# Moving the first RMSNorm behind the first product, and merging two score matmuls, in a two-layer hybrid decoder on one core

## The chip, the cores and the metric

The kernel runs on one core of one Trainium2 chip. The metric is device time in microseconds (us) of one execution. The engines are the TensorE (PE in the profile, its weight loads PEld), the VectorE (DVE), the ScalarE (ACT), GpSimd (POOL) and the SyncE (SP), which here only issues DMA transfers. Each engine works its instructions in the order in which the kernel wrote them, and waits where an operand or a buffer is not ready.

## The reference

Two layers, one sequence of 256 tokens, 1024 channels, float32. Cut to what matters here:

```python
for l in range(DEPTH):                               # DEPTH = 2
    h = rmsnorm(x, norm_mix_g[l])                    # x * rsqrt(mean(x*x) + eps) * g
    x = x + mixer_block(h, w_in[l], ...)             # mLSTM and sliding-window attention, gated
    h = rmsnorm(x, norm_mlp_g[l])
    x = x + square(relu(h @ w_up[l])) @ w_down[l]
return rmsnorm(x, final_norm_g)

# mixer_block
proj = h @ w_in                                      # 6664 columns: mqk, mv, mo, gates mi/mf, aq, ak, av, ga, gb
mqk = silu(causal_conv(mqk, conv_w, conv_b))         # q and k of the mLSTM
logf = log_sigmoid(mf + b_fgate)                     # and its running sums and maxima: the gates
hm = mlstm(mq, mk, mv, mi + b_igate, logf)           # normed per head, times sigmoid(mo)
# attention: 16 query heads of 64, 4 key/value heads, window 128, a sink per head, a T5 bias
logits = q @ k.T / 8 + bias                          # masked to 0 <= distance < 128
m = max(max(logits), sink); p = exp(logits - m)
ha = p @ v / (sum(p) + exp(sink - m))
y = sigmoid(ga) * (hm @ w_branch_m) + sigmoid(gb) * (ha @ w_branch_a)
return y @ w_out
```

A factor that is one number per token, such as the norm's rsqrt, can be applied to a product's rows after the product as well as to x before it. The factor g is one number per channel and has to be applied before.

## The kernel before

**Precision.** Float32 operands of the large products are split in two parts, hi (a cast, on ACT) and lo (what is left, a subtraction on DVE). A product is then three matmuls: hi by hi, hi by lo, lo by hi. This holds for the weights (`pump_hi`, `pump_lo`, lines 142 and 123) and for the activations (`evac_split`, line 311).

**Weights.** They stream from memory in pieces of 128 rows by 1024 columns (512 KB). SP loads a piece into one of 4 `raw` buffers (`pump_dma`, line 114), ACT casts it into a hi buffer, DVE writes lo and thereby frees the raw buffer for the load of the piece four later. There are 7 pairs of hi and lo buffers; a pair is free again when PE has used it.

**Slots.** The products are cut into slots, mostly 24 matmuls of 256 columns or 12 of 512 columns. `run_slots` (line 191) writes the instructions of one slot after the other, and this sets the order on every engine: first the side work hung to the slot with `at`; then the hi casts of pieces up to four ahead of what the slot needs (`limits` can hold that back); then the work hung with `at_late`; the lo parts; the work hung with `at_last`; then the slot's matmuls (units); then what was hung behind it with `after`.

The stages of a layer's mixer are, with their slots: mv (8 slots, the values of the mLSTM), kv (4: keys, values and gate columns), aq (8: queries), qk (8), mo (8), gb, ga (8 each), then the branches. `s_mv`, `s_kv`, `s_aq`, `s_qk` are their first slots. In an `xs` unit (line 211) tokens stand in the output's partitions, in a `ws` unit (line 226) channels. A group's head and tail say in which order its units run: "k" uses up one weight piece per slot, all four output banks in turn; "t" runs the first token tile over two pieces at a time and then the second tile; "b" finishes one output bank per slot; "p" pairs them.

**The start** (`setup_start`, line 401, and `first_norm`, line 526). SP loads X's first tile of 128 tokens in two halves, the g row, three weight pieces, X's second tile, a fourth piece, and then eleven small tensors, some of them broadcast to 128 partitions by the load. PE runs dummy matmuls on zeros meanwhile (`N_WARM`). Squares of a tile are summed on ACT and DVE, POOL takes the power -1/2, DVE scales the tile, PE transposes it in blocks of 128, and ACT and DVE write the hi and lo parts with g as a factor per partition, block by block. The first product (mv) takes the first tile first.

**The gates.** `gates1` computes log sigmoid with a chain of small operations on POOL, with one reciprocal on DVE in it. `gates2`, `gates2b`, `gates2c` transpose the result on PE and scan it on DVE; `gates3` transposes back and writes the gate columns. In POOL's order `k_split` (the lo part of the keys) comes ahead of `gates1`.

**The heads.** Each of 16 heads runs in four steps. `att1` (line 827): the scores, four matmuls, then bias and minimum on DVE, exponentials on ACT. `att2`: sums and reciprocal on DVE, scaling on POOL. `att3`: transposes on PE and their copy. `att4`, for four heads: the product with the values. `heads_at` (line 884) gives the slot of `att1`, counted from `s_qk`; `att2` comes one slot later, `att3` three. The four score matmuls of a head are:

```python
nc.tensor.matmul(sp[:, 0:P], q[:, 0:P], kh[:, gk, 0:P], start=True, stop=False, ...)
nc.tensor.matmul(sp[:, 0:P], q[:, 0:P], kl[:, gk, 0:P], start=False, stop=True, ...)
nc.tensor.matmul(sp[:, P : 3 * P], q[:, P:T], kh[:, gk, :], start=False, stop=False, ...)
nc.tensor.matmul(sp[:, P : 3 * P], q[:, P:T], kl[:, gk, :], start=False, stop=True, ...)
```

Tiles named `pa` and `pb` in the profile are PSUM banks, four of each.

Of the kernel before, what the change touches and what calls it, by code (L numbers as in the profile page):

```python
# [11 lines left out]
F32 = mybir.dt.float32  # L12
# [5 lines left out]
P = 128  # L18
# [24 lines left out]
def trunk(ctx: ExitStack, tc: tile.TileContext, x, norm_mix_g, w_in, conv_w, conv_b, b_igate, b_fgate,  # L43
# [43 lines left out]
    def piece(w, kt, c0):  # L87
        def load(raw):
            nc.sync.dma_start(raw[:, :1024], w[kt * P : (kt + 1) * P, c0 : c0 + 1024])

        pieces.append((load, 1024))
        return len(pieces) - 1
# [21 lines left out]
    def pump_dma():  # L114
        j = n_dma[0]
        if j < len(pieces):
            raws[j] = wp.tile([P, 1040], F32, tag="raw", bufs=N_RAW, name=nm("raw"))
            pieces[j][0](raws[j])
            n_dma[0] += 1
# [3 lines left out]
    def pump_lo():  # L123
# [5 lines left out]
        los.clear()  # L129

# [256 lines left out]
    N_WARM = (26, 16, 8)  # L387

    def small_loads():
# [4 lines left out]
        for l in range(DEPTH):  # L394
            nc.sync.dma_start(gb_bias[:, l, 0:4], b_igate[l].partition_broadcast(P))
            nc.sync.dma_start(gb_bias[:, l, 4:8], b_fgate[l].partition_broadcast(P))
            nc.sync.dma_start(sink[:, l, :], attn_sinks[l].partition_broadcast(P))
            nc.sync.dma_start(rows[40 * l : 40 * l + 32, :], conv_w[l].rearrange("j (m c) -> (j m) c", c=P))
            nc.sync.dma_start(rows[40 * l + 32 : 40 * l + 40, :], conv_b[l].rearrange("(m c) -> m c", c=P))

    def setup_start():
        grow = big8()[:8, 0, 0:P]
        nc.sync.dma_start(X[:, 0, 0:512], xv[:, 0, 0:512])
        nc.sync.dma_start(X[:, 0, 512:], xv[:, 0, 512:])
        nc.sync.dma_start(grow, norm_mix_g[0].rearrange("(k c) -> k c", c=P))
        for i in range(N_RAW):
            if i == 3:
                nc.sync.dma_start(X[:, 1, :], xv[:, 1, :])
            pump_dma()
# [7 lines left out]
        pw = psA()  # L417
        for _ in range(N_WARM[0]):
            nc.tensor.matmul(pw[:, :P], mask, mask, start=True, stop=True)
        pg = psA()  # L420
        nc.tensor.transpose(pg[:, :8], grow, ident[:8, :8])
        S0["gcol"] = const.tile([P, KT], F32, name="gcol")
        S0["pg"], S0["pw"] = pg, pw
        for _ in range(N_WARM[1]):
            nc.tensor.matmul(pw[:, :P], mask, mask, start=True, stop=True)

    def setup_small():
# [6 lines left out]
        nc.scalar.copy(Rs, z[:, 0:384])  # L434
        for r in (0, 32):
            nc.gpsimd.affine_select(out=z[r : r + 32, 0:4], in_=z[r : r + 32, 0:4], pattern=[[-1, 4]],
                                    compare_op=ALU.not_equal, fill=1.0, base=0, channel_multiplier=1)
        nc.scalar.copy(sel, z[:, 0:4])

    def setup_cols():  # L440
        pt = psB()
        nc.tensor.transpose(pt[:, :80], S0["rows"], ident[:80, :80])
        nc.vector.tensor_copy(cw, pt[:, :80])
        pt = psB()
        nc.tensor.transpose(pt[:16, :NB_BUCKETS], S0["rb"], ident[:NB_BUCKETS, :NB_BUCKETS])
        nc.vector.tensor_scalar(nsink, sink, -1.0, None, op0=ALU.mult)
        rbT = const.tile([16, NB_BUCKETS], F32, name="rbT")
        nc.vector.tensor_scalar(rbT, pt[:16, :NB_BUCKETS], -1.0, None, op0=ALU.mult)
# [77 lines left out]
    def first_norm(st, xtag, nxt):  # L526

        xh, xl = st["hT"] = xT_tiles(xtag)
        N = [Norm(0), Norm(1)]
        gcol, xn, pts = S0["gcol"], {}, {}  # L530

        def scale(tt, hf):
            xn[tt, hf] = tmp()
            nc.vector.tensor_scalar(xn[tt, hf], X[:, tt, hc(hf)], N[tt].r[:, :1], None, op0=ALU.mult)

        def tr(tt, hf):
            pts[tt, hf] = psB()
            for j in range(4):
                nc.tensor.transpose(pts[tt, hf][:, j * P : (j + 1) * P], xn[tt, hf][:, j * P : (j + 1) * P], ident)

        def hi(tt, ks):
            for k in ks:
                nc.scalar.activation(xh[:, k, tt * P : (tt + 1) * P], pts[tt, k // 4][:, k % 4 * P : (k % 4 + 1) * P],  # L543
                                     AF.Copy, scale=gcol[:, k : k + 1])

        def lo(tt, ks):
            for k in ks:
                s = slice(tt * P, (tt + 1) * P)
                nc.vector.scalar_tensor_tensor(xl[:, k, s], pts[tt, k // 4][:, k % 4 * P : (k % 4 + 1) * P],
                                               gcol[:, k : k + 1], xh[:, k, s].bitcast(F32), op0=ALU.mult,  # L550
                                               op1=ALU.subtract)

        N[0].square(0)
        N[0].square(1, "dve")
        N[0].rstd()
        nc.scalar.copy(gcol, S0["pg"][:, :8])
        pump_hi(0, 0)
        scale(0, 0)
        tr(0, 0)
        for _ in range(N_WARM[2]):  # L560
            nc.tensor.matmul(S0["pw"][:, :P], mask, mask, start=True, stop=True)
        pump_lo_part(0, 512)
        hi(0, (0, 1))
        lo(0, (0, 1))
# [3 lines left out]
        hi(0, (2, 3))  # L568
        pump_lo()
        lo(0, (2, 3))  # L570
        pump_hi(0, 2)
        N[1].square(0)
        N[1].square(1)
        pump_lo()
        N[1].rstd()
        scale(0, 1)
        pump_hi(0, 3)
        scale(1, 0)
        pump_lo()
# [581 lines left out]
```

## Time and profile before

| | |
|---|---|
| time, median of 3 runs | 882.46 us (881.98 to 882.62) |
| the profiled execution: its time, its span | 882.83 us, 881.1 us |
| mean granted clock of the TensorE | 0.995 |
| busy: PE, DVE, ACT, POOL | 867.6, 566.5, 468.8, 123.1 us |
| bytes read from memory, mean rate over the span | 153.23 MB, 175 GB/s |
| first matmul of the first product | at 8.89 us of the span |

A line of the timeline reads: start and duration in us, engine, line of the kernel, operation, output tile and input tiles, shapes, how many instructions are merged in it; in brackets the idle time before it and what ended that. A line of a group has the count, then the busy time in all, the mean duration in ns, and the idle time before with its releasers. A line of stages has the stretch in us from the span's start, its length, then busy time and count of PE, PEld, DVE, ACT and POOL, and at the end the granted clock, the share of the DMA engines and GB/s. PE's durations overlap one another, so the spacing of a stream of matmuls is read from the difference of their starts.

### The profile page before, as it was taken

What the parts mean: (1) busy time and instruction counts of PE and PEld (TensorE: products, weight loads), DVE (VectorE), ACT (ScalarE), POOL (GpSimd) and SP (SyncE); (2) the same over time, 40 slices, a digit from 0 to 9 for tenths busy, and PEclk for the clock granted to TensorE, in tenths of its full rate; (3) what the DMA queues carried; (4) which work ended last, traced back from release to release, by engine and by line L of the source; (5) the groups of instructions that cost most, each with busy time, mean ns of one, the idle gap of its engine ahead of it and who ended that gap; (6) DMA issues with size and microseconds to landing.
All of it is one profiled execution on the core that took longest, in us unless ns stands there. A gap on an engine that the chain in (4) does not pass through costs nothing.

```text
span 881.1 us, 15013 instructions
## 1 busy us (share of the span) xinstructions
PE 867.6 (98%) x5929; PEld 792.4 (90%) x5929; DVE 566.5 (64%) x897; ACT 468.8 (53%) x771; POOL 123.1 (14%) x164
## 2 busy tenths in 40 slices
PE   8999999999999999999999999999999999999996
PEld 6899879999989999998889998899998899999985
DVE  5758869666666654546474687776667764737363
ACT  5657866554355554544355567765634453636252
POOL 1361722120000000000001454122000000000000
PEclk9999999999999999999999999999999999999998
DMA  6875445445556737474655453454564466555521
GB/s 217 288 244 190 123 142 164 146 145 163 173 192 209 242 124 253 128 245 128 226 169 192 148 182 109 161 168 144 154 222 158 145 227 222 196 187 188 194 96 48
DMA packets 50711, 155.28 MB, mean 176 GB/s; under 512 B 7912, under 2 KB 10192, under 8 KB 50640
## 3 DMA queue, kind: packets, MB, share of 16 engines
q1 hardware_dynamic: 49456, 150.69, 52.6%
q0 software_dynamic: 896, 3.17, 1.1%
q8 instruction: 46, 0.75, 0.3%
q10 hardware_dynamic: 288, 0.46, 0.1%
q14 instruction: 25, 0.20, 0.1%
HBM read 153.23 MB, written 1.07 MB: 175 GB/s over the span
## 4 chain that ended last, share of the span: by engine, by line
PE 87%; DVE 5%; issue 2%; DMA 2%; ACT 2%; SPq 1%; POOL 1%; POOLq 0%; DVEq 0%; ACTq 0%
PE pa L220 11%; PE pa L221 11%; PE pa L222 11%; PE pa L235 11%; PE pa L234 11%; PE pa L236 11%; PE pb L235 5%; PE pb L234 5%; PE pb L236 5%; DMA raw<-in_w_in 2%; DVE lo L127 2%; PE pb L322 1%; PE pb L860 1%; PE pb L879 1%; PE pb L918 1%
## 5 line engine op out<-in xcount | busy, mean ns | idle before, releaser
L127 DVE TENSOR_TENSOR lo<-raw,hi 128x1024 fp32r<-128x1024 f32 (+1 forms) x276 | 331.5, 1224 | 136.0 <-ACT hi L152 133.5
L152 ACT CAST hi<-raw 128x1024 fp32r<-128x1024 f32 (+1 forms) x280 | 286.1, 1049 | 186.3 <-PE pa L222 49.7
L234 PE MATMUL pa<-xh,hi 128*128 128x256 f32 x864 | 246.6, 285 | 0.0
L235 PE MATMUL pa<-xl,hi 128*128 128x256 f32 x864 | 242.7, 281 | 0.0
L236 PE MATMUL pa<-xh,lo 128*128 128x256 f32 x864 | 241.6, 280 | 0.0
L234 PEld LDWEIGHTS pa<-xh,hi 128*128 128x128 f32 x864 | 162.6, 188 | 1.2 <-ACT vm L605 0.4
L235 PEld LDWEIGHTS pa<-xl,hi 128*128 128x128 f32 x864 | 163.1, 189 | 0.3
L236 PEld LDWEIGHTS pa<-xh,lo 128*128 128x128 f32 x864 | 162.8, 188 | 0.0
L220 PE MATMUL pa<-hi,xh 128*128 128x512 f32 (+1 forms) x384 | 150.5, 392 | 1.5 <-ACT xh L543 1.4
L221 PE MATMUL pa<-lo,xh 128*128 128x512 f32 (+1 forms) x384 | 148.4, 386 | 0.2 <-DVE lo L127 0.2
L222 PE MATMUL pa<-hi,xl 128*128 128x512 f32 (+1 forms) x384 | 148.3, 386 | 0.0
L234 PE MATMUL pb<-xh,hi 128*128 128x256 f32 x384 | 107.6, 280 | 0.0
L235 PE MATMUL pb<-xl,hi 128*128 128x256 f32 x384 | 107.6, 280 | 0.0
L236 PE MATMUL pb<-xh,lo 128*128 128x256 f32 x384 | 107.3, 280 | 0.0
L222 PEld LDWEIGHTS pa<-hi,xl 128*128 128x128 f32 x384 | 72.5, 189 | 15.6
L220 PEld LDWEIGHTS pa<-hi,xh 128*128 128x128 f32 x384 | 72.5, 189 | 14.8 <-ACT xh L543 1.6
L221 PEld LDWEIGHTS pa<-lo,xh 128*128 128x128 f32 x384 | 72.6, 189 | 13.9 <-DVE lo L127 0.6
L349 POOL TENSOR_TENSOR sm<-sm,mhalf 128x1 f32<-128x1 f32 x9 | 6.5, 725 | 499.8 <-DVE sm L348 499.8
L235 PEld LDWEIGHTS pb<-xl,hi 128*128 128x128 f32 x384 | 72.4, 188 | 1.7
L234 PEld LDWEIGHTS pb<-xh,hi 128*128 128x128 f32 x384 | 72.2, 188 | 1.8
L236 PEld LDWEIGHTS pb<-xh,lo 128*128 128x128 f32 x384 | 72.3, 188 | 0.0
L220 PE MATMUL pa<-hi,b 128*128 128x512 f32 x124 | 48.8, 394 | 0.0
(210 smaller groups left out, 979.2 us busy)
## 6 DMA issues: line engine op xcount, KB each, us to landing
raw<-in_w_in SPq DMA_DIRECT2D x104, 512.0 KB, 4.5
raw<-in_w_up SPq DMA_DIRECT2D x64, 512.0 KB, 4.7
raw<-in_w_down SPq DMA_DIRECT2D x64, 512.0 KB, 4.3
raw<-in_w_branch_a SPq DMA_DIRECT2D x16, 512.0 KB, 3.5
raw<-in_w_branch_m SPq DMA_DIRECT2D x16, 512.0 KB, 4.1
raw<-in_w_out SPq DMA_DIRECT2D x16, 512.0 KB, 4.5
b<-ed SPq DMA_DIRECT2D x4, 512.0 KB, 5.4
g<-in_mlstm_norm_g POOLq DMA_DIRECT2D x2, 512.0 KB, 6.1
```

Of the source, the lines that this page charges most:

```text
L127: nc.vector.tensor_tensor(lo[:, :n], raw[:, :n], hi[:, :n].bitcast(F32), op=ALU.subtract)
L152: nc.scalar.copy(hi[:, :n], raw[:, :n])
L220: nc.tensor.matmul(b, xh[:, kt, s], wh[:, c], start=first, stop=False)
L221: nc.tensor.matmul(b, xh[:, kt, s], wl[:, c], start=False, stop=False)
L222: nc.tensor.matmul(b, xl[:, kt, s], wh[:, c], start=False, stop=last)
L234: nc.tensor.matmul(o, wh[:, c], xh[:, kt, :], start=first and half == 0, stop=False, skip_group_check=True)
L235: nc.tensor.matmul(o, wh[:, c], xl[:, kt, :], start=False, stop=False, skip_group_check=True)
L236: nc.tensor.matmul(o, wl[:, c], xh[:, kt, :], start=False, stop=last, skip_group_check=True)
L322: nc.tensor.transpose(pt[:, j * P : (j + 1) * P], src[:, j * P : (j + 1) * P], ident)
L860: nc.tensor.transpose(tp[:, j * P : (j + 1) * P], L[:, j * P : (j + 1) * P], ident)
L879: nc.tensor.matmul(o, va[:, 0, vs], PT[:, 0:T], start=(h < h0 + 2), stop=False, skip_group_check=True)
L918: nc.tensor.matmul(pn[:, :257], W[:, tt * P : (tt + 1) * P], vm[:, 0, h, :], start=True, stop=(tt == 0))
```

## The change

It has four parts.

1. **The start.** The first product of layer 0 runs on x times g, without the rsqrt. SP loads the left halves of both tiles of X first, then weight piece 0 in two loads, pieces 1 and 2, the right halves, piece 3, and six small tensors in place of eleven; g comes over ACT's queue. PE transposes x itself, one DVE instruction multiplies four blocks by g, one ACT and one DVE instruction write hi and lo (`hU`). The right halves follow in slots 1 and 2 of the product, the squares and the power in slots 2 and 3. The product's head is "k" with the second and third unit of the first slot swapped. The evacuation of the values multiplies by the rsqrt of the token. From slot 6 on, PE spreads the rsqrt as a row over the partitions, and x times g is multiplied by it: the first half of the channels in slot 6, the second behind the values' evacuation. This gives the `hT` that all later products of the layer use.
2. **Setup.** The gate biases and sinks are loaded as one row and spread by a matmul; `setup_small` moves from slot 2 to 8 of the product's count, with its ACT copies in slot 10, `setup_cols` from 4 to 5, the bias loads and reversals two slots earlier. The keys' bank of kv is allotted first.
3. **Gates.** `k_split` comes behind `gates1` in the same slot; `gates2`, `2b`, `2c` come two slots earlier, `gates3` one, and its columns are copied by ACT in place of DVE.
4. **Heads.** hi and lo parts of the keys are one tile `k2`, and the first two score matmuls become one, with both parts as its moving operand and two blocks of the bank as its output; one more DVE instruction adds the second block. The first eight heads run one a slot from slot 0.

```diff
-    N_WARM = (26, 16, 8)
+    N_WARM = (22, 0, 20)
...
+        nc.scalar.dma_start(grow, norm_mix_g[0].rearrange("(k c) -> k c", c=P))
+        for tt in range(2):
+            nc.sync.dma_start(X[:, tt, 0:512], xv[:, tt, 0:512])
+        pump_dma(2)
+        pump_dma()
+        pump_dma()
+        for tt in range(2):
+            nc.sync.dma_start(X[:, tt, 512:], xv[:, tt, 512:])
+        pump_dma()
         small_loads()
...
+        uh, ul = st["hU"] = xT_tiles("xb")
+        xg = big8((P, KT, T))
...
+        def times_g(tt, hf):
+            nc.vector.tensor_tensor(xg[sl(tt, hf)], pts[tt, hf].rearrange("p (k t) -> p k t", k=4),
+                                    gcol[:, 4 * hf : 4 * hf + 4].unsqueeze(2).to_broadcast([P, 4, P]), op=ALU.mult)
+        def hi(tt, hf):
+            nc.scalar.copy(uh[sl(tt, hf)], xg[sl(tt, hf)])
+        def lo(tt, hf):
+            nc.vector.tensor_tensor(ul[sl(tt, hf)], xg[sl(tt, hf)], uh[sl(tt, hf)].bitcast(F32), op=ALU.subtract)
...
+        times_g(0, 0)
+        hi(0, 0)
+        times_g(1, 0)
+        pump_hi_part(0, 512)
+        lo(0, 0)
+        hi(1, 0)
         pump_lo_part(0, 512)
+        lo(1, 0)
+        pump_hi_part(512, 1024)
         pump_lo_part(512, 1024)
         pump_lo_done()
         pump_hi(0, 1)
         pump_lo()
+        def rest(tt):
+            tr(tt, 1)
+            times_g(tt, 1)
+            hi(tt, 1)
+            lo(tt, 1)
+        def norm(tt):
+            N[tt].square(0)
+            N[tt].square(1)
+            N[tt].rstd()
+        u = slots[nxt][0]
+        u[1], u[2] = u[2], u[1]
+        limits[nxt] = 1
+        for i in range(1, 5):
+            limits[nxt + i] = 1 + i
+        for tt in range(2):
+            slots[nxt + 1 + tt][0].insert(2, call(lambda tt=tt: rest(tt)))
+            at_last(nxt + 2 + tt, lambda tt=tt: norm(tt))
+        def rows():
+            pr = psB()
+            for tt in range(2):
+                nc.tensor.matmul(pr[:, tt * P : (tt + 1) * P], N[tt].r[:, 0:1].to_broadcast([P, P]), ident, start=True,
+                                 stop=True, skip_group_check=True)
+            S0["R"] = tmp()
+            nc.scalar.copy(S0["R"][:, 0:T], pr[:, 0:T])
+            st["hT"] = xT_tiles(xtag)
+        def normed(c):
+            s = (slice(None), slice(4 * c, 4 * c + 4), slice(None))
+            nc.vector.tensor_tensor(xg[s], xg[s], S0["R"][:, 0:T].unsqueeze(1).to_broadcast([P, 4, T]), op=ALU.mult)
+            evac_split(xg[s], st["hT"][0][s], st["hT"][1][s])
+        at(nxt + 6, rows)
+        at(nxt + 6, lambda: normed(0))
...
-        s_mv = xs_group(st, "mv", "hT", w, MV0, head="t")
+        s_mv = xs_group(st, "mv", "hT" if l else "hU", w, MV0, head="t" if l else "k")
...
+            if l == 0:
+                r = S0["r"][tt]()
+                if hf:
+                    nc.vector.tensor_scalar(o, i, r, None, op0=ALU.mult)
+                else:
+                    nc.scalar.activation(o, i, AF.Copy, scale=r)
...
         by_bank(s_mv, mv_evac)
+        if l == 0:
+            after(s_mv + 7, lambda: S0["normed"](1))
...
-        at(s_kv, lambda: st.update({("kv", 0): psA(), ("kv", 1): psA(), "kk": psA()}))
+        at(s_kv, lambda: st.update({"kk": psA(), ("kv", 0): psA(), ("kv", 1): psA()}))
...
-        at(s_aq + 1, k_split)
...
-            nc.vector.tensor_copy(cols, pcv)
+            nc.scalar.copy(cols, pcv)
...
         at_late(s_aq + 1, gates1)
-        at_last(s_aq + 8, gates2)
-        at_last(s_aq + 9, gates2b)
-        at_last(s_aq + 10, gates2c)
-        at(s_aq + 14, gates3)
+        at_late(s_aq + 1, k_split)
+        at_last(s_aq + 6, gates2)
+        at_last(s_aq + 7, gates2b)
+        at_last(s_aq + 8, gates2c)
+        at(s_aq + 13, gates3)
...
-            nc.tensor.matmul(sp[:, 0:P], q[:, 0:P], kh[:, gk, 0:P], start=True, stop=False, skip_group_check=True)
-            nc.tensor.matmul(sp[:, 0:P], q[:, 0:P], kl[:, gk, 0:P], start=False, stop=True, skip_group_check=True)
-            nc.tensor.matmul(sp[:, P : 3 * P], q[:, P:T], kh[:, gk, :], start=False, stop=False, skip_group_check=True)
-            nc.tensor.matmul(sp[:, P : 3 * P], q[:, P:T], kl[:, gk, :], start=False, stop=True, skip_group_check=True)
+            nc.tensor.matmul(sp.rearrange("p (a t) -> p a t", a=4)[:, 0:4:3, :], q[:, 0:P], k2[:, :, gk, 0:P],
+                             start=True, stop=True, skip_group_check=True)
+            nc.tensor.matmul(sp[:, P : 3 * P], q[:, P:T], k2[:, 0, gk, :], start=False, stop=False, skip_group_check=True)
+            nc.tensor.matmul(sp[:, P : 3 * P], q[:, P:T], k2[:, 1, gk, :], start=False, stop=True, skip_group_check=True)
...
+            nc.vector.tensor_tensor(L[:, 0:P], sp[:, 384:512], biasT[:, h, P:T], op=ALU.add)
+            nc.vector.tensor_tensor_reduce(L[:, 0:P], sp[:, 0:P], L[:, 0:P], 1.0, nsk, op0=ALU.add,
...
-            if h in (0, 14):
+            if h == 0:
                 nc.vector.tensor_copy(PT, tp[:, 0:384])
...
-        heads_at = (2, 3, 3, 4, 5, 6, 6, 7, 8, 9, 10, 12, 14, 20, 20, 22)
+        heads_at = (0, 1, 2, 3, 4, 5, 6, 7, 8, 9, 10, 12, 14, 20, 20, 22)
...
-            at(s_mv + 2, setup_small)
-            at(s_mv + 4, setup_cols)
+            at(s_mv + 8, setup_small)
+            at(s_mv + 10, setup_copies)
+            at(s_mv + 5, setup_cols)
             for q in range(4):
-                at(s_mv + 12 + q, lambda q=q: load_bias(q))
-                at(s_mv + 18 + q, lambda q=q: setup_bias(q))
+                at(s_mv + 10 + q, lambda q=q: load_bias(q))
+                at(s_mv + 16 + q, lambda q=q: setup_bias(q))
```

More of the change, by code (lines that the diff above doesn't have):

```diff
@@ L87, in piece, with load @@
     def piece(w, kt, c0):
-        def load(raw):
-            nc.sync.dma_start(raw[:, :1024], w[kt * P : (kt + 1) * P, c0 : c0 + 1024])
+        def load(raw, parts=1):
+            for a in range(0, 1024, 1024 // parts):
+                b = a + 1024 // parts
+                nc.sync.dma_start(raw[:, a:b], w[kt * P : (kt + 1) * P, c0 + a : c0 + b])
         pieces.append((load, 1024))
@@ L117, in pump_dma @@
             raws[j] = wp.tile([P, 1040], F32, tag="raw", bufs=N_RAW, name=nm("raw"))
-            pieces[j][0](raws[j])
+            pieces[j][0](raws[j], *parts)
             n_dma[0] += 1
@@ L129, in pump_lo, with pump_hi_part @@
         los.clear()
+    def pump_hi_part(a, b):
+        j = n_split[0] - (1 if a else 0)
+        if not a:
+            pc[j] = tuple(wp.tile([P, 1040], F32R, tag=t, bufs=N_SPL, name=nm(t)) for t in ("hi", "lo"))
+            los.append(j)
+            n_split[0] += 1
+        nc.scalar.copy(pc[j][0][:, a:b], raws[j][:, a:b])
     def pump_lo_part(a, b):
@@ L416, in setup_start @@
         nc.vector.memset(mask, 0.0)
-        pw = psA()
+        pw = S0["pw"] = psA()
         for _ in range(N_WARM[0]):
             nc.tensor.matmul(pw[:, :P], mask, mask, start=True, stop=True)
[L420 to L425, printed above, removed]
+        S0["grow"] = grow
     def setup_small():
@@ L526, in first_norm @@
     def first_norm(st, xtag, nxt):
-        xh, xl = st["hT"] = xT_tiles(xtag)
+        uh, ul = st["hU"] = xT_tiles("xb")
+        xg = big8((P, KT, T))
         N = [Norm(0), Norm(1)]
[L530 to L534, printed above, removed]
+        gcol = const.tile([P, KT], F32, name="gcol")
+        pts = {}
         def tr(tt, hf):
@@ L538, in tr @@
             for j in range(4):
[L539 to L561, printed above, removed]
+                c = hf * 512 + j * P
+                nc.tensor.transpose(pts[tt, hf][:, j * P : (j + 1) * P], X[:, tt, c : c + P], ident)
+        def sl(tt, hf):
+            return (slice(None), slice(4 * hf, 4 * hf + 4), slice(tt * P, (tt + 1) * P))
@@ L562, in first_norm @@
+        nc.vector.tensor_copy(gcol, pg[:, :8])
+        for tt in range(2):
+            tr(tt, 0)
+            for _ in range(N_WARM[1 + tt]):
+                nc.tensor.matmul(S0["pw"][:, :P], mask, mask, start=True, stop=True)
+        times_g(0, 0)
[4 more added lines that the diff above has]
+        hi(1, 0)
         pump_lo_part(0, 512)
-        hi(0, (0, 1))
-        lo(0, (0, 1))
+        lo(1, 0)
+        pump_hi_part(512, 1024)
         pump_lo_part(512, 1024)
```

78 lines of the change are left out of this document (32 added, 46 removed).

## The prediction

> **What bounds the kernel now.** I read the page first, then the waits of the TensorE (PE), the groups by shape, and stretches of the timeline.
>
> ```profile
> span 881.1 us, 15013 instructions
> PE 867.6 (98%) x5929; PEld 792.4 (90%) x5929; DVE 566.5 (64%) x897; ACT 468.8 (53%) x771; POOL 123.1 (14%) x164
> ```
>
> PE is busy 98% of the span, so two things alone can shorten it: less PE work, or fewer of the holes that are left. The profiled execution took 882.83 us, 1.7 us more than its span and 0.4 us above the median of 882.46; the sum below is made against 882.8. The holes lie in two places. The first is the start:
>
> ```profile
> 4.11 0.69 DVE L344 CUSTOM_DVE_ANT_0 tmp<-X 128x512 f32<-128x512 f32 x1 [3.12 <-DMA X<-in_x]
> ...
> 7.53 1.04 ACT L152 CAST hi<-raw 128x1024 fp32r<-128x1024 f32 x1 [2.68 <-DMA raw<-in_w_in]
> ...
> 8.89 0.77 PE L220 MATMUL pa<-hi,xh 128*128 128x512 f32 x1 [1.43 <-ACT xh L543]
> ...
> 8.99 1.04 ACT L152 CAST hi<-raw 128x1024 fp32r<-128x1024 f32 x1
> ...
> 10.44 1.06 ACT L152 CAST hi<-raw 128x1024 fp32r<-128x1024 f32 x1
> ...
> 11.66 0.63 ACT L342 ACTIVATE tmp<-X 128x512 f32<-128x512 f32 x1 [0.17 <-DMA X<-in_x]
> ...
> 14.69 0.35 SPq L89 DMA_DIRECT2D raw<-in_w_in  x1
> ...
> 34.89 0.40 PE L220 MATMUL pa<-hi,xh 128*128 128x512 f32 x1
> 35.12 0.40 PE L221 MATMUL pa<-lo,xh 128*128 128x512 f32 x1
> 35.36 0.40 PE L222 MATMUL pa<-hi,xl 128*128 128x512 f32 x1
> ```
>
> The second half of X's first tile is there at 4.11, weight piece 0 at 7.53, piece 1 by 8.99, piece 2 by 10.44, X's second tile at 11.66. The first real matmul starts at 8.89, the last of product 1 at 35.36. At 0.23 us each its 96 matmuls need 22.1 us; they take 35.36 + 0.23 - 8.89 = 26.7. Part of the difference is the clock:
>
> ```profile
> 5.57:8.98 3.41, 1.71 (x22) 1.35 (x19) 0.86 (x2) 1.45 (x3) 0.21 (x1) 1.00 0.99 340
> 8.98:12.40 3.42, 3.42 (x8) 2.66 (x9) 3.42 (x8) 3.25 (x8) 0.00 (x0) 0.51 0.78 297
> ```
>
> After a stretch with PE busy for 1.71 of 3.41 us, the granted clock (the third figure from the end) is 0.51, and only 8 matmuls fit into 3.42 us.
>
> The second place is the attention heads, when the third product ("qk", slots qk+0 on) has begun:
>
> ```profile
> 92.12 0.28 PE L835 MATMUL pb<-kl,b 128*128 128x256 f32 x1
> 93.17 0.33 PE L832 MATMUL pb<-kh,b 128*128 128x128 f32 x1 [0.77 <-ACT guard L737]
> ...
> 522.54 0.28 PE L835 MATMUL pb<-kl,b 128*128 128x256 f32 x1
> 523.06 0.33 PE L832 MATMUL pb<-kh,b 128*128 128x128 f32 x1 [0.25 <-ACT guard L737]
> ```
>
> From start to start 1.05 and 0.52 us pass where 0.12 would do (a stream's spacing, shown below): 1.3 us lost over both layers.
>
> **The merged scores.** One head, and the stream behind it:
>
> ```profile
> 507.13 0.22 PE L832 MATMUL pb<-kh,b 128*128 128x128 f32 x1
> ...
> 507.59 0.28 PE L234 MATMUL pa<-xh,hi 128*128 128x256 f32 x1
> 507.71 0.28 PE L235 MATMUL pa<-xl,hi 128*128 128x256 f32 x1
> ```
>
> Four matmuls take 507.59 - 507.13 = 0.46 us; 256 columns in a stream take 0.12. The two of 128 columns become one of 256, so a head is three of 0.12, 0.35, and 32 heads save 32 x 0.11 = 3.5 us. The trace has no matmul with a moving operand in two blocks, or an output in two blocks. Bounds: 0.46 again (no gain), and 0.31, as if the merged one cost a third less than 0.12 (4.8 us). I take 0.35, since it is one instruction of the stream's width.
>
> **The start.** SP's order of bytes stays X (0.5 MB), pieces 0, 1, 2, rest of X, piece 3; X's first two pieces are now the left halves of both tiles, and piece 0 comes in two loads. So I keep the landings above and put piece 0's first half midway between 4.11 and 7.53, at 5.8. Durations beside the 1.04 of a weight piece on ACT:
>
> ```profile
> L127 DVE TENSOR_TENSOR lo<-raw,hi 128x1024 fp32r<-128x1024 f32 x268 | 321.7, 1223 | 129.8 <-ACT hi L152 127.3 <-PE pa L222 0.4
> L314 DVE TENSOR_TENSOR xl<-pb,xh 128x512 fp32r<-128x512 f32 x32 | 22.1, 691 | 39.9 <-ACT xh L313 39.9
> L313 ACT CAST xh<-pb 128x512 fp32r<-128x512 f32 x32 | 18.8, 587 | 50.3 <-PE pb L322 35.9 <-PE pb L880 14.5
> ```
>
> No square, mean or power stands before the product any more: X goes through transposes, one product with g (0.69), ACT's half (0.59) and DVE's half (0.69), done by 6.4. ACT's half of a half piece takes 0.55, so the first matmul can start at 5.8 + 0.6 = 6.4, 2.5 us earlier. With the "k" order piece 1 is needed one slot later: ACT 8.99 to 10.0, DVE to 11.25. From there 83 matmuls remain: 83 x 0.23 = 19.1, and 1.6 us for the transposes and small matmuls between them and a late piece 4. Product 1 ends near 32.0 instead of 35.6: 3.6 us.
>
> The Trainium skill ("TensorE: Matmul & The Clock Gate", Part 1) lets the clock fall after an idle window of about 3.4 us that runs freely; the two windows above agree, and by it one half-busy window in the new start would cost up to 1.7 us (half of 3.41). The sum would stay, since PE then only waits less at the hand-over below; rival A would shrink by it.
>
> **The hand-over to kv.** What the norm did before the product now follows, on ACT and DVE, and both run in order. Slots 1 to 4 may split one piece each; between them stand X's right halves (DVE 0.69 + 0.69, ACT 0.59) and four squares on ACT (0.63 each, the 11.66 row). On ACT, step by step: piece 2 to 11.4, half of X to 14.3, piece 3 to 15.3, squares to 16.6, half of X to 18.1, piece 4 to 19.2, squares to 20.4, piece 5 to 21.5; DVE ends piece 5 at 22.7. That frees the buffer for piece 9, kv's second.
>
> ```profile
> raw<-in_w_in SPq DMA_DIRECT2D x104, 512.0 KB, 4.5
> ```
> ```profile
> 36.40 1.28 DVE L603 COPY vm<-pa 128x512 f32<-128x512 f32 x2
> ...
> 37.13 0.39 PE L220 MATMUL pa<-hi,xh 128*128 128x264 f32 x1
> ```
>
> 4.5 us later, at 27.3, it lands; ACT 28.4, DVE 29.6. Next in order comes the first normed half: DVE product 1.22 (30.8), ACT 1.05 (31.9), DVE 1.22 (33.1), then pieces 10 and 11 on DVE (35.5), and only now the evacuations of product 1: ACT's first bank is free at 34.5, DVE's at 36.2. PE, done at 32.0, waits for them. Before, kv's third bank was had at 37.13; now at 36.25. So of 3.6 us about **0.9 to 1.0 remains**. The second normed half (1.22 + 1.05 + 1.22 behind two evacuations of 0.64) ends at 40.4, just before kv's third slot at 40.9: covered by 0.5 us; without that cover it is lost one for one. Bounds for the start: 3.6 gained (no hand-over wait) and 1.0 lost (piece 9 lands 2 us later).
>
> The rest of the setup is costed at nothing. SP has 6 small loads where 11 held back piece 4 until 14.69; POOL's constants, ACT's two copies and the reversed bias loads need be ready only in the aq product, two slots of 2.8 us (24 matmuls of 0.12) or more behind their new places; if the bias table is not yet in memory when SP comes to load it, the weight loads queued behind wait too, four pieces (11 us) ahead of use. The new order of kv's banks is worth 0.4 us at most.
>
> **Gates and heads.** Layer 1, whose rows have no setup in them:
>
> ```profile
> 480.05 5.85 POOL L643 TENSOR_TENSOR kl<-tmp,kh 64x512 fp32r<-64x512 f32 x4 [30.66 <-ACT kh L642]
> 486.00 0.26 POOL L679 TENSOR_SCALAR sm<-sm 128x8 f32<-128x8 f32 x1
> ...
> 496.93 0.20 POOL L693 TENSOR_TENSOR lf<-sm,sm 128x8 f32<-128x8 f32 x1
> ...
> 501.05 0.27 PE L698 MATMUL pb<-ident,lf 128*4 128x128 f32 x1
> ```
>
> The gate chain takes 486.00 to 497.13, 11.1 us. Put ahead of the split of k (5.85) it can start at about 482.2, when ACT's exponential is done, and end at 493.3; PE's transposes of it, two slots (5.6) earlier, come at 495.4: 2.1 us to spare. The split of k then ends at 499.2, the first scores come at 501.05. DVE, whose reciprocal no longer stands behind the split, is freed in a slot where nothing waits for it.
>
> Then DVE, at qk+0:
>
> ```profile
> 502.48 1.39 DVE L659 SCALAR_TENSOR_TENSOR b<-pa,b 64x512 fp32r<-64x512 f32 x2 [1.43 <-ACT b L656]
> 503.90 3.50 DVE L127 TENSOR_TENSOR lo<-raw,hi 128x1024 fp32r<-128x1024 f32 x3
> ...
> 510.39 0.31 DVE L839 CUSTOM_DVE_ANT_0 L<-pb,biasT,nsink 128x128 f32<-128x128 f32 x1
> ...
> 511.05 2.34 DVE L127 TENSOR_TENSOR lo<-raw,hi 128x1024 fp32r<-128x1024 f32 x2
> ...
> 513.32 0.21 DVE L719 TENSOR_SCALAR b<-b 4x128 f32<-4x128 f32 x1
> ...
> 515.00 0.16 DVE L851 TENSOR_TENSOR sm<-sm 128x2 f32<-128x2 f32 x1
> ...
> 515.56 0.61 POOL L853 TENSOR_SCALAR L<-L,sm 128x128 f32<-128x128 f32 x1 [18.43 <-DVE sm L852]
> 516.16 0.92 POOL L854 TENSOR_SCALAR L<-L,sm 128x256 f32<-128x256 f32 x1
> ```
>
> A head's first DVE part was 511.05 - 510.39 = 0.66; the added sum of 128 columns is not in the trace, by the nearest row (0.31) 0.3, at least 0.15. New order: evacuation to 503.9, head 0 to 504.9, three splits (3.5) to 508.4, the third gate step (1.7, 513.32 to 515.00) to 510.1, head 0's sums to 510.4, POOL (0.2 later, 1.5 long) to 512.1. PE reaches head 0's transposes after three slots of 2.8 + 0.35: 501.05 + 9.45 = 510.5. It **waits 1.6 us** there, in each layer, 3.2 in all. Later heads have 0.5 to 2 us to spare. The 1.3 us above go, since the gate columns no longer wait for DVE. Net +1.9; bounds -1.3 (no new wait) and +4.
>
> **The sum:** -3.5 (scores) - 1.0 (start) + 1.9 (heads) - 0.2 (banks, half of the bound) = -2.8: 880.0 in a profiled execution, 882.5 - 2.8 = **879.7** against the median.
>
> **Rivals.** A: the hand-over wait is not there, because pieces and halves come 2 or 3 us earlier than I add up; the whole 3.6 stay: 877.1. For it: 0.1 us of overlap between neighbours in a row of splits (3 in 3.50, not 3.67), which I left out. Against it: the buffer chain through piece 9. B: the merged matmul costs what the pair did: 883.2. For it: its operand and output come in two blocks, as no row has. C, slower: POOL becomes the heads' bound.
>
> ```profile
> 518.91 1.67 POOL L853 TENSOR_SCALAR L<-L,sm 128x128 f32<-128x128 f32 x1
> ```
>
> The same step took 0.61 above; here a DVE split runs beside it. With heads one a slot and their sums behind splits, each head can lose 1.06. Heads 1 to 7 have slack of 0.5 to 2; if on average 0.5 is lost for 14 heads, it is 7 us: 886.7. It decides from 0.33 a head on ((2.8 + 1.8) / 14). Against it: DVE's work per slot, 0.96 + 0.3 + 1.2 = 2.5, is under PE's 3.5. The Trainium skill ("SBUF — State Buffer", Who interferes with whom) says a DVE instruction with two SBUF inputs holds off a GpSimd read; the 1.67 agrees.
>
> **How the numbers follow.** Mine 0.5 (own range 877.5 to 882), A 0.22, B 0.13, C 0.10, something else near no change 0.05. A measurement tells 0.2%, 1.8 us, from no change. Faster (below 880.7): three quarters of mine and A, 0.60. Slower (above 884.2): C, a part of B and of mine, 0.15. Same: 0.25. Range 875.5 to 884.5: A whole, B, and no C.
>
> **What would show it.** Start: PE's first product matmul near 6.4, its last near 32, no row of half clock between; kv's first matmul after a wait for an evacuation at 34 to 36 (if it starts at 32, A). Scores: three matmuls in 0.35 us (0.46 is B). Heads: PE waits for POOL at the first head's transposes in both layers, 1 to 2 us; no wait for the gate columns; L853 mostly 0.6 (1.6 is C). Wrong altogether if PE waits for the gate transposes, or the weight splits fall behind in aq.

## The result, and the profile after

The changed kernel takes **877.64 us** (median of 4 runs, 877.18 to 877.98) against 882.54 us (881.98 to 882.62) for the kernel before: a ratio of 0.9947, 95% interval 0.9936 to 0.9959, or 4.9 us less. 879.7 was forecast. One execution of 2191.4 us, in experiment 6, is a slow one and is not used in the comparisons. The profiled execution took 877.81 us. From the page of the changed kernel:

```profile
span 876.0 us, 14994 instructions
...
PE 862.2 (98%) x5895; PEld 788.2 (90%) x5895; DVE 577.0 (66%) x918; ACT 469.6 (54%) x768; POOL 119.0 (14%) x165
```

The span is 5.1 us shorter and PE is busy for 5.4 us less. The waits of PE over 0.3 us that are new (waiter, what it waited for, us in total, times, longest):

```profile
PE pa L244 <- ACT vm L645: 1.4, 1, 1.4
PE pb L908 <- POOL L L902: 1.2, 2, 0.6
...
PE pb L908 <- POOL L L901: 0.9, 2, 0.5
PE pa L230 <- DVE vm L643: 0.4, 1, 0.4
```

The first and last are the hand-over from product 1 to kv, the other two the first head's transposes, once in each layer. The wait for the gate columns (before: L832 behind "guard") has no row any more. The start in the timeline, with the hand-over:

```profile
5.89 1.85 PE L577 MATMUL pa<-mask 128*128 128x128 bf16 x20
6.10 0.61 ACT L139 CAST hi<-raw 128x512 fp32r<-128x512 f32 x1
...
7.56 0.48 PE L230 MATMUL pa<-hi,xh 128*128 128x512 f32 x1
...
8.25 1.05 ACT L162 CAST hi<-raw 128x1024 fp32r<-128x1024 f32 x1 [0.24 <-DMA raw<-in_w_in]
...
26.59 1.06 ACT L162 CAST hi<-raw 128x1040 fp32r<-128x1040 f32 x1 [1.52 <-PE pb L616]
...
31.05 2.02 ACT L162 CAST hi<-raw 128x1040 fp32r<-128x1040 f32 x2
...
31.91 0.40 PE L232 MATMUL pa<-hi,xl 128*128 128x512 f32 x1
...
32.32 2.38 DVE L129 TENSOR_TENSOR lo<-raw,hi 128x1040 fp32r<-128x1040 f32 x2
32.97 1.26 ACT L645 ACTIVATE vm<-pa,sm 128x512 f32<-128x512 f32 x2
...
33.70 0.38 PE L244 MATMUL pa<-xh,hi 128*128 128x256 f32 x1 [1.40 <-ACT vm L645]
...
34.63 1.40 DVE L643 TENSOR_SCALAR vm<-pa,sm 128x512 f32<-128x512 f32 x2
...
35.43 0.39 PE L230 MATMUL pa<-hi,xh 128*128 128x264 f32 x1 [0.39 <-DVE vm L643]
```

The first product matmul starts at 7.56, because the dummy matmuls of L577 fill PE until about then; its cast was done at 6.7 (without them it starts at 6.76, experiment 6). Product 1 ends at 31.91 + 0.23 = 32.1 us. Then PE waits, since ACT (31.05) and DVE (32.32) split two more weight pieces ahead of the evacuations. ACT's copy of the keys, the first thing behind kv, ties the two starts together:

```profile
47.18 0.59 ACT L626 COPY tmp<-pa 128x512 f32<-128x512 f32 x1 [3.23 <-PE pa L236]
```
```profile
45.47 0.59 ACT L672 COPY tmp<-pa 128x512 f32<-128x512 f32 x1 [2.92 <-PE pa L246]
```

Of 3.5 us at the end of product 1, 1.7 are left at the end of kv. A single pair of traces is rough here: this copy stands at 46.10 to 47.18 in the five traces with the old start (experiments 2 to 5 and the kernel before) and at 44.79 to 45.47 in the four with the new one (experiments 1, 7 and 11 and the changed kernel). By their means the start is worth 1.5 us at this point.

Layer 1's gates and first heads after the change:

```profile
488.44 0.20 POOL L738 TENSOR_TENSOR lf<-sm,sm 128x8 f32<-128x8 f32 x1
488.60 5.35 POOL L689 TENSOR_TENSOR k<-tmp,k 64x512 fp32r<-64x512 f32 x4
...
491.50 0.27 PE L743 MATMUL pb<-ident,lf 128*4 128x128 f32 x1
...
503.97 0.28 PE L879 MATMUL pb<-k,b 128*128 128x256 f32 x1
...
504.20 0.28 PE L882 MATMUL pb<-k,b 128*128 128x256 f32 x1
...
505.97 0.55 DVE L769 TENSOR_TENSOR Rs<-b,Rs 4x384 fp32r<-4x384 f32 x1 [0.25 <-ACT Rs L768]
506.53 0.16 DVE L899 TENSOR_TENSOR sm<-sm 128x2 f32<-128x2 f32 x1
...
507.10 0.61 POOL L901 TENSOR_SCALAR L<-L,sm 128x128 f32<-128x128 f32 x1 [13.15 <-DVE L L886]
...
507.76 0.33 PE L908 MATMUL pb<-ident,L 128*128 128x128 f32 x1 [0.45 <-POOL L L901]
508.66 0.44 PE L908 MATMUL pb<-ident,L 128*128 128x128 f32 x2 [0.58 <-POOL L L902]
```

The score matmuls stand 0.12 us apart. Head 0's sums (506.53) stand on DVE behind the third gate step, which ends at 505.97 + 0.55 = 506.52. PE's spacing shows 1.44 us lost at 507.02 to 508.66, and 1.46 in layer 0.

In layer 0 another 1.5 us come between kv and the last branch product, in layer 1 0.6 us. But 1.4 us of the 5.1 arise where the change has no work at all (middle and end of the layers). That was not in the forecast.

### The profile page after: what moved, and what is told of

The parts are those of the page before. It is cut to its first block, busy times and chain, and to the rows that moved or that the text cites. A ratio compares the mean times of both kernels' runs of the same rounds, so it can differ in the third digit from the quotient of the medians.

```text
span 876.0 us, 14994 instructions
## 1 busy us (share of the span) xinstructions
PE 862.2 (98%) x5895; PEld 788.2 (90%) x5895; DVE 577.0 (66%) x918; ACT 469.6 (54%) x768; POOL 119.0 (14%) x165
## 4 chain that ended last, share of the span: by engine, by line
PE 91%; DVE 4%; issue 2%; ACT 1%; POOL 1%; POOLq 0%; DVEq 0%; ACTq 0%
PE pa L231 12%; PE pa L230 12%; PE pa L232 12%; PE pa L244 11%; PE pa L245 11%; PE pa L246 11%; PE pb L245 5%; PE pb L244 5%; PE pb L246 5%; PE pb L908 1%; DVE lo L129 1%; PE pb L332 1%; PE pb L927 1%; PE pb L966 1%; POOL sm L359 1%
## 5 line engine op out<-in xcount | busy, mean ns | idle before, releaser
L231 PE MATMUL pa<-lo,b 128*128 128x512 f32 x124 | 48.9, 395 | 0.0
```

The costliest lines, as they stand in the source:

```text
L231: nc.tensor.matmul(b, xh[:, kt, s], wl[:, c], start=False, stop=False)
```

## The experiments

All times are medians; each group of runs stood beside 15 to 23 runs of the kernel before (882.17, 882.25 and 882.38 us for the three groups).

**1. The start and the setup alone.** The changed kernel with `k_split`, the gate steps, the copy of the gate columns, the score matmuls and the heads' slots as before:

```diff
-        heads_at = (0, 1, 2, 3, 4, 5, 6, 7, 8, 9, 10, 12, 14, 20, 20, 22)
+        heads_at = (2, 3, 3, 4, 5, 6, 6, 7, 8, 9, 10, 12, 14, 20, 20, 22)
...
```

> The changed kernel with its scores, gates and heads as before; only the start is changed. Theory (the terms add up, the start keeps what kv shows): kv's last evacuation comes 1.7 us earlier than before, and so does the end: 880.8 against 882.5. Rival one (what the untouched stages seem to give, 1.3 us over the span, belongs to the start's shift): about 879.5. Rival two (the start's gain is given back at the heads of layer 0, which wait for something that does not move with it): 882.5.

878.66 us, ratio 0.9965 (0.9953 to 0.9977): **3.5 us** faster, more than any of the three figures; rival one is nearest, and what it says of the untouched stages is taken up in experiment 5.

**2. Scores, gates and heads alone.** The kernel before with those parts of the diff (and the bias tables' loads two slots earlier, which the early heads need).

> The kernel before with the merged scores, the gate columns in slot 5 and the heads one a slot, and no change of the start. Theory: 32 heads save 0.105 us each (3.4), the old waits go (1.4 in layer 0, 0.5 in layer 1), and PE waits 1.45 us at the first head's transposes in each layer (2.9): 882.5 - 3.4 - 1.9 + 2.9 = 880.1. Rival one (the new wait in layer 0 came from the earlier start): no such wait in layer 0, 878.7. Rival two (POOL or DVE fall behind in the heads): 883 or more.

880.80 us, ratio 0.9985 (0.9976 to 0.9993): 1.4 us faster, and 1.4 + 3.5 is the 4.9 us of the whole change. The waits, from its trace:

```profile
PE pb L861 <- POOL L L854: 1.3, 2, 0.8
PE pb L861 <- POOL L L855: 1.2, 2, 0.6
```

Both layers have the new wait without the earlier start: rival one is out.

**3. The merged scores alone.**

```diff
-            nc.tensor.matmul(sp[:, 0:P], q[:, 0:P], kh[:, gk, 0:P], start=True, stop=False, skip_group_check=True)
-            nc.tensor.matmul(sp[:, 0:P], q[:, 0:P], kl[:, gk, 0:P], start=False, stop=True, skip_group_check=True)
+            nc.tensor.matmul(sp.rearrange("p (a t) -> p a t", a=4)[:, 0:4:3, :], q[:, 0:P], k2[:, :, gk, 0:P],
+                             start=True, stop=True, skip_group_check=True)
...
+            nc.vector.tensor_tensor(L[:, 0:P], sp[:, 384:512], biasT[:, h, P:T], op=ALU.add)
```

> The kernel before with the merged score matmuls and DVE's added sum alone; gates and heads stand where they stood. Theory: three matmuls in place of four take 0.105 us less at each of 32 heads, and DVE's sum of 0.28 us a head lies beside PE's work: 882.5 - 3.4 = 879.1. Rival (DVE's sum is not covered where two heads share a slot, and PE waits for the heads' transposes): 0.28 x 6 heads a layer or more, 881 to 883.

884.43 us (882.52 to 884.67), ratio 1.0019 (1.0010 to 1.0028): **slower**, by 2.3 us. Its waits:

```profile
PE pb L832 <- ACT guard L737: 1.8, 2, 0.9
PE pb L832 <- DVE sm L842: 1.2, 2, 0.6
```

With two heads in a slot, DVE's added sums push its other work back: the gate columns are copied at 523.98 where it was 522.63 before, and PE waits 0.9 us for them where it waited 0.25. That DVE's sum is not covered is the rival's mechanism, though PE waits more for the gate columns and for DVE's reading of earlier scores (the two rows above) than for the heads' transposes. By the spacing of PE's matmuls the waits cost some 3.3 us more than before over both layers, which eats the 3.4 us. There is more behind it, in the stages around that place of layer 1 (granted clock third from the end):

```profile
521.80:525.20 3.40, 1.87 (x13) 1.41 (x12) 3.29 (x13) 2.20 (x9) 2.12 (x4) 1.00 0.62 169
525.20:528.60 3.40, 3.40 (x19) 3.40 (x18) 2.92 (x12) 2.97 (x11) 1.46 (x2) 0.51 0.47 147
528.60:532.00 3.40, 3.40 (x30) 3.40 (x30) 1.79 (x6) 2.25 (x7) 2.41 (x4) 0.99 0.45 147
```

Two waits of about 1 us within 3.4 us leave PE busy for 1.87, and the next 3.4 us are granted half the clock: 19 matmuls where the stretch after has 30, so some 1.2 to 1.7 us are lost on top of the waits. Layer 0 of the same trace has the same pair of waits, and there the clock stays:

```profile
91.78:95.19 3.41, 1.90 (x13) 1.50 (x14) 3.34 (x14) 2.41 (x9) 2.27 (x4) 1.00 0.65 172
95.19:98.60 3.41, 3.41 (x31) 3.41 (x31) 2.88 (x12) 3.35 (x13) 1.47 (x3) 1.00 0.53 156
```

The Trainium skill ("TensorE: Matmul & The Clock Gate", Part 1) has the clock fall after an idle window of about 3.4 us; this trace agrees on the length, but the window before the fall in layer 1 was not idle. So PE's busy share alone does not tell whether the clock falls. Three of the ten executions took 882.5 to 883.1 us, the others 884.2 to 884.7; the two at 882.57 and 883.13 were granted 0.998 on average, the third 0.996, and the slower ones 0.995 or 0.996. So those two seem to have been without the fall, and they are no faster than the kernel before either.

**4. The new order alone,** with four score matmuls a head; the gate steps stand where the change puts them:

```diff
-        at(s_aq + 1, k_split)
+        at_late(s_aq + 1, k_split)
...
-        heads_at = (2, 3, 3, 4, 5, 6, 6, 7, 8, 9, 10, 12, 14, 20, 20, 22)
+        heads_at = (0, 1, 2, 3, 4, 5, 6, 7, 8, 9, 10, 12, 14, 20, 20, 22)
```

> The kernel before with the gate columns in slot 5 and the heads one a slot, but with four score matmuls a head as before. The kernel with both gained 1.4 us, the one with the merged scores alone lost 2.2. Theory (the merged matmuls save PE 3.4 us wherever no head waits, and alone they lost it again to waits that the reorder removes): the reorder alone costs its own two waits of 1.45 us less the old 1.9 us, so 882.2 + 1.0, between 882.2 and 884.2. Rival (the two edits add up): 880.8 + 882.2 - 884.4 = 878.6.

882.89 us, ratio 1.0006 (0.9997 to 1.0014): nothing gained, as the theory had it. So one part is worth +2.3, the other +0.6, and both together -1.4. **They don't add**: the merged matmul pays only when the heads stand one a slot, and then 2.0 us (882.89 to 880.80, each beside its own runs of the kernel before) of the 3.4 that it saves PE; the wait at the first head's transposes is longer with it (3.3 us over both layers in the trace of experiment 2, some 2.2 here).

**5. Where the tiles lie.** Kernels with the changed start ran the untouched stages a little faster. Here the kernel before sets unused tiles aside, and nothing else is changed:

```diff
+        const.tile([P, 4], F32, name="z2")
+        xT_tiles("xb"), big8(), tmp()
         xh, xl = st["hT"] = xT_tiles(xtag)
```

By the program's allocations the weight tiles then start 32 bytes further up in each partition, the big buffers too, and the two transposed-x tiles and the heads' tiles lie in other places, as in the changed kernel. No instruction is added.

> The kernel before with no change of its work: four tiles that nothing uses are set aside at the start, so that the tiles of the transposed x, the weight pieces and the big buffers come to lie where they lie in the changed start. Theory (in the stages that the change does not touch, the kernels with the changed start run matmuls 0.7% closer because of where their tiles lie in SBUF): matmuls there at 0.1176 and 0.2309 us in place of 0.1184 and 0.2331, and 1.5 us faster, 880.7. Rival (something else in the start does it): 882.2, with the spacing of before.

881.05 us, ratio 0.9986 (0.9977 to 0.9994): 1.2 us faster with the same work. One stage without any edit, from the last transposes of layer 0's mLSTM output to those at the layer's residual sum, in the kernel before, then the placed one, then the changed one:

```profile
206.63 0.38 PE L322 MATMUL pb<-ident,b 128*128 128x128 f32 x2
...
260.39 0.38 PE L322 MATMUL pb<-ident,tmp 128*128 128x128 f32 x2
```
```profile
205.84 0.38 PE L322 MATMUL pb<-ident,b 128*128 128x128 f32 x2
...
259.35 0.49 PE L322 MATMUL pb<-ident,tmp 128*128 128x128 f32 x3
```
```profile
203.42 0.38 PE L332 MATMUL pb<-ident,b 128*128 128x128 f32 x2
...
256.81 0.38 PE L332 MATMUL pb<-ident,tmp 128*128 128x128 f32 x2
```

53.76, 53.51 and 53.39 us. The granted clock reads 1.00 in this stage in all three. So the places of the tiles account for 0.25 of the 0.37 us here. The same holds for the two long stretches from the last of these transposes to the copy of layer 1's keys, and from the same transposes in layer 1 to the last matmul: together 507.28 us in the kernel before and within 0.01 of it in experiments 2 to 4, which keep the old start and its places; 506.45 in the placed one; 505.92 in the changed one. The places make 0.8 of these 1.4 us. Which of the tiles does it, by what mechanism, and what makes the rest, stays open.

**6. Without the dummy matmuls ahead of the first product:** `N_WARM = (22, 0, 0)` in place of `(22, 0, 20)`.

> The changed kernel without the 20 dummy matmuls between the transposes of X's second tile and the first product matmul. Theory (the hand-over to kv, not PE, sets the end of the start): PE may start as early as 6.6 us, and then has one stretch at half clock that costs it up to 1.7 us, but it waits 1.9 us at the hand-over anyway: within 0.4 us of the changed kernel, 877.6. Rival one (PE sets it): 1.7 us slower, 879.3. Rival two (an earlier first matmul counts): up to 1 us faster, 876.6.

878.42 us, ratio 0.9955 (0.9942 to 0.9967) against 0.9947 (0.9936 to 0.9959) for the changed kernel: 0.8 us slower by the medians, but the two intervals overlap. The trace has a stretch at half clock, which the changed kernel's hasn't:

```profile
9.50:11.30 1.80, 1.80 (x6) 1.41 (x5) 1.18 (x1) 1.59 (x2) 0.00 (x0) 0.50 0.91 355
```

Its first product matmul starts at 6.76, 0.8 earlier, and the last at 32.91, 1.0 later; by the end of kv 0.6 is left, because PE waits less for the evacuations. Neither end of the expectation was met: the hand-over takes back only part. The one execution at 876.88 us was granted 0.997 on average, the four at 878.28 to 878.80 us 0.995; it fits rival two, an earlier start without the half clock, but it is a single one.

**7. The third gate step one slot later,** so that head 0's sums stand ahead of it on DVE: `at_last(s_aq + 9, gates2c)` in place of 8.

> The changed kernel with the third gate step one slot later, so that DVE sums head 0 ahead of it. Theory (PE's wait of 1.45 us at head 0's transposes, in each layer, comes from this step standing ahead on DVE): the wait goes, 877.6 - 2.9 = 874.7. Rival one (POOL's two scalings decide, not DVE): no more than 0.3 us faster. Rival two (what waits for the gate columns waits in its place): about 877.6.

875.38 us, ratio 0.9922 (0.9910 to 0.9935): 2.3 us faster than the changed kernel. The median lies between two pairs, 874.52 and 874.56, 876.20 and 876.63; the trace is that of 876.20. In it layer 1's wait is gone:

```profile
505.05 0.61 POOL L901 TENSOR_SCALAR L<-L,sm 128x128 f32<-128x128 f32 x1 [11.66 <-DVE L L886]
505.65 0.92 POOL L902 TENSOR_SCALAR L<-L,sm 128x256 f32<-128x256 f32 x1
...
506.78 0.49 PE L908 MATMUL pb<-ident,L 128*128 128x128 f32 x3
```

POOL is done at 506.57, before PE comes. Layer 0 still loses 1.05 us. There DVE is later in this trace, with its first rows of head 0 at 72.74 where the changed kernel's stood at 71.88. What holds it back is read from these rows, and not tested:

```profile
57.99 7.12 POOL L689 TENSOR_TENSOR k<-tmp,k 64x512 fp32r<-64x512 f32 x4
...
59.84 4.12 DVE L129 TENSOR_TENSOR lo<-raw,hi 128x1024 fp32r<-128x1024 f32 x2 [2.19 <-ACT hi L162]
```

Two weight splits take 4.12 us beside POOL's split of k, where two take 2.4 elsewhere (32.32 above), and they start late: ACT's cast ahead of them had waited 2.4 us for its weight piece. What sets the two pairs of times apart is not known.

**8. Pieces 10 and 11 behind the evacuations:**

```diff
+        limits[nxt + 6] = limits[nxt + 7] = 9
...
-            evac_split(xg[s], st["hT"][0][s], st["hT"][1][s])
+            hi, lo = st["hT"][0][s], st["hT"][1][s]
+            if c:
+                pump_hi(nxt + 8, 10)
+            nc.scalar.copy(hi, xg[s])
+            if c:
+                pump_lo()
+            nc.vector.tensor_tensor(lo, xg[s], hi.bitcast(F32), op=ALU.subtract)
```

> The changed kernel with weight pieces 10 and 11 split behind the first product's evacuations, inside the second normed half. Theory (PE's wait at the hand-over, 1.56 us for ACT's evacuation and 0.55 for DVE's, comes from these pieces standing ahead of the evacuations): 1.2 to 1.8 us faster than the changed kernel, 876.1. Rival one (the normed x half itself is late): the first wait stays, 877.6. Rival two (the second normed half and pieces 10 and 11 are then late for kv's third slot): 877 to 878.

878.11 us (876.60 to 879.45), ratio 0.9948 (0.9936 to 0.9960): near the changed kernel, but the median falls between two groups of three. In the trace the theory's wait is gone and kv ends 1.5 us earlier; but DVE at layer 0's first head is no earlier than it was, so PE waits there 3.1 us in place of 1.46, and the half clock follows:

```profile
77.80:81.20 3.40, 1.25 (x9) 1.06 (x10) 2.39 (x14) 2.09 (x7) 1.86 (x3) 1.00 0.67 258
81.20:84.60 3.40, 3.40 (x18) 3.40 (x18) 3.40 (x8) 2.06 (x7) 1.17 (x2) 0.51 0.20 29
```

This profiled execution took 879.45 us, and the two others near it were, like it, granted 0.995 on average. The other three took 876.6 to 876.9 us at 0.997 or 0.998, so they seem to have been without the half clock; their traces were not taken. They lie near the theory's 876.1, 0.7 to 1.0 us under the changed kernel.

**9 and 10. Both edits, and then layer 0's first eleven heads one slot later.**

```diff
         heads_at = (0, 1, 2, 3, 4, 5, 6, 7, 8, 9, 10, 12, 14, 20, 20, 22)
+        if l == 0:
+            heads_at = (1, 2, 3, 4, 5, 6, 7, 8, 9, 10, 11, 12, 14, 20, 20, 22)
```

> The changed kernel with both edits: the third gate step one slot later, and pieces 10 and 11 split behind the first product's evacuations. Theory (the hand-over's 1.4 us and layer 1's 1.2 us are gained; in layer 0 the first head waits for DVE, which POOL's split of k and late weight pieces hold back, so that it can take the earlier start back): 873.5 to 874.5 where the first head of layer 0 does not wait longer, up to 876.5 where it does. Rival (the hand-over's gain is always lost at layer 0's first head): 875.4, as with the third gate step alone.

> The same, and in layer 0 the first eleven heads one slot later (1, 2, ... 11), layer 1 unchanged. Theory (layer 0's first head waits because DVE is a little behind there, not because of anything that moves with the head): one slot is 2.8 us, more than the wait, so PE no longer waits there and the hand-over's gain stays: 873.0, at least 1 us under the kernel without this edit. Rival (the late heads 10 and 11 then meet the third gate step, the gate columns and the memory heads): no gain, 874 to 876.5.

875.48 us, ratio 0.9921 (0.9908 to 0.9935) with both edits: by the medians no better than with the gate step alone, as the rival of the first had it. In the traces kv ends 1.7 us earlier than in experiment 7, and 0.7 of that is left at the transposes of layer 0's second head (82.03 against 82.75); the wait at the first is 1.7 us in place of 1.05. With the later heads **874.42 us**, ratio 0.9907 (0.9893 to 0.9920), 1.06 under the kernel without this edit as the theory had it, though not the 873.0 named; all four of its executions (872.80 to 875.17) lie under all five of the other (875.31 to 875.71). PE's waits of its trace show why: a shorter wait at the first head is left, and a new one for the evacuation of the queries, on DVE too.

```profile
PE pa L244 <- DVE b L712: 0.7, 1, 0.7
PE pb L915 <- POOL L L909: 0.4, 1, 0.4
```

It is the fastest of all kernels here, 3.2 us under the changed kernel and 8.0 under the one before.

**11. The split of k ahead of the gate chain again:** `at(s_aq + 1, k_split)` in place of the line behind `gates1`.

> The changed kernel with POOL's split of k ahead of the gate chain again, as in the kernel before. Theory (the gates can come two slots earlier only because the split of k gave up its place): the gate chain ends 5.4 to 7.1 us later, at about 65.5 and 494.0 us where PE comes at 62.95 and 491.5, so PE waits 2.5 us in each layer; DVE gains on PE by that, and up to 1.45 us of the wait at the first head goes: 2 to 5 us slower than the changed kernel, 880 to 882.5. Rival (the gate chain has slack enough in either order): 877.6.

881.15 us, ratio 0.9993 (0.9982 to 1.0004): 3.5 us of the 4.9 are lost. One row says where:

```profile
PE pb L743 <- POOL lf L738: 3.2, 2, 1.6
```

PE waits for the gate chain in both layers, 1.6 us where 2.5 was expected, and the wait at the first head stays as it was (1.2 and 1.0 us in all): DVE's rows of head 0 move back with PE's scores.

## Why the prediction was right, and where it was not

The forecast of 879.7 lies 2.1 us above the result; the range and the sign were right. Point by point:

- **Merged scores, -3.5.** The price of the matmul was right: three in 0.35 us behind a stream (503.97 to 504.20 and 0.12), 0.11 us less for each head. B is out. But "a head is three of 0.12, 0.35, and 32 heads save 32 x 0.11" took this as a term of its own. Alone it cost 2.3 us (experiment 3). It is a term only together with the order of the heads, and there it is worth 2.0 us (experiment 4), not 3.5.
- **Gates and heads, +1.9.** The wait of 1.6 us in each layer was named with its place and cause, and measured 1.46 and 1.44; the gate columns' waits went. Experiment 7 shows the cause, third gate step ahead of head 0's sums, for layer 1. In layer 0 the changed kernel's rows stand as in layer 1 (head 0's sums 6.1 us behind DVE's first row of that head in both), but experiment 7 took only a part of the wait away, and the rest of the cause is argued. Scores and heads together: -1.6 forecast, -1.4 measured (experiment 2). That the sum came out is in part luck: with the old order of heads the scores alone lost time, and with four matmuls the new order alone gained nothing; the prediction added the two terms as if each stood for itself.
- **Gate chain.** "2.1 us to spare" was 2.9 (488.64 against 491.50), and experiment 11 shows that its place in POOL's order carries this.
- **The start, -1.0, and the banks, -0.2.** Product 1 was to end at 32.0 and ended at 32.1, though it began at 7.56 and not 6.4: the dummy matmuls, left out of the working, delayed its first matmul, but piece 1 (cast at 8.25) was there 0.7 us before the 8.99 that I had used, so little stalled later. The hand-over wait came as described, in the same order, each step 0.7 to 0.9 us earlier than added up (piece 9 on ACT to 27.65 and not 28.4, ACT's evacuation at 32.97 where I had it end its first bank at 34.5). So the term measured -1.7 at the end of kv against the trace shown, -1.5 by the means of all. The term was mis-sized, and the landings that it was worked from are a likely source, not a shown one: piece 1 was cast at 8.06 to 8.76 in the four traces with the new start. The order of kv's banks was not run apart. Rival A, no wait, is out, although its 877.1 is nearer to the result than mine.
- **The clock at the start.** The prediction gave the stretch at half clock as part of why product 1 takes 26.7 us. What it cost does not show: in experiment 4's trace the old start begins its product at 8.95 with no half clock and starts the last matmul at 35.37, where the kernel before, at half clock, had 8.89 and 35.36. Six executions of the kernel before that were granted 0.994 or 0.995 on average have a median of 882.4 us, the 49 at 0.997 or 0.998 one of 882.2.
- **What was left out.** Experiment 1 puts the whole start at -3.5. In its trace 1.2 us of the gain arise in the two long stretches of experiment 5, which the start's work does not touch; the places of the tiles account for 0.8 of that, and the kernel with the places alone was 1.2 us faster. "The rest of the setup is costed at nothing" did not hold for its allocations. What remains of the 3.5 fits the earlier end of kv and a shorter wait for the gate columns (0.7 us in all, 1.0 before), within the spread of the start.
- **C, slower.** POOL's two scalings got faster, not slower: groups of the changed kernel, mean in ns behind the busy time.

```profile
L902 POOL TENSOR_SCALAR L<-L,sm 128x256 f32<-128x256 f32 x32 | 29.7, 927 | 0.0
L901 POOL TENSOR_SCALAR L<-L,sm 128x128 f32<-128x128 f32 x32 | 23.8, 744 | 123.8 <-DVE sm L899 36.9 <-DVE sm L900 33.2 <-DVE L L886 29.5
...
L886 DVE TENSOR_TENSOR L<-pb,biasT 128x128 f32<-128x128 f32 x32 | 9.0, 282 | 0.1
```

Before, the scaling of 128 columns took 828 ns (L853) and that of 256 took 1080 (L854). The added sum took 0.28 us, 0.3 forecast.

So scores and heads came out nearly as summed, -1.6 against -1.4, though neither term held by itself. The start was too small, -1.2 against about -1.5 to -1.7 at the end of kv and -3.5 in all; what the sum missed most is a gain in stages that have no edit.

## What to carry to other kernels

Take a matmul away from PE only after asking which engine gets work for it: here 3.4 us of PE time were worth less than nothing until DVE's work was spread one head a slot, and 2.0 us then. Count waits by where they fall as well as by their length: two of about 1 us within 3.4 us cost another 1.2 to 1.7 us in clock in one layer, and nothing more in the other. Where a median falls between two groups of executions, look at the groups and at their clocks before comparing it. And when a stage without an edit changes its pace, test the places of the tiles with unused ones before explaining it by the work.

## What the runs showed of the hardware

- The granted clock was halved for about 3.4 us after stretches in which PE was busy for 1.87 of 3.40 us (experiment 3, layer 1), 1.25 of 3.40 (experiment 8) and 1.71 of 3.41 (the start before). It stayed full after 2.37 of 3.40 (the changed kernel's wait in layer 1), but also after 1.90 of 3.41 (experiment 3, layer 0), 1.87 of 3.41 (experiment 11, 61.30 to 64.71) and 1.75 of 3.41 (experiment 4, 5.25 to 8.66). So between 1.75 and 1.90 the busy time does not decide it, and what does stays open.
- The same work took 53.51 us in place of 53.76 in one stage, at a granted clock of 1.00, 506.45 in place of 507.28 over the two long stretches, and 1.2 us less over the whole kernel, when its tiles lay elsewhere.
- POOL's split of k took 7.12 us beside DVE's weight splits (experiment 7, layer 0) and 5.35 us where DVE ran none (the changed kernel, layer 1), and two DVE splits took 4.12 us in place of 2.4: both sides were held up. In experiment 11, where POOL's split stands earlier, the two DVE splits in that place took 1.22 and 1.23 us. The Trainium skill ("SBUF — State Buffer", Who interferes with whom) describes a pair of ports that the two engines share as an exclusive lock, and has a DVE instruction with two SBUF inputs, as the split is, contend with a GpSimd instruction that reads SBUF; these numbers agree, and show the loss on either side.
- A matmul with its moving operand in two blocks 4 KB apart, and its output in two blocks of one bank, was spaced like one with contiguous operands: 0.12 us.
